# Weight splits of the differential attention made during the retention and kept in DRAM, with small steps moved between engines: a diffusion backbone on one core

## The chip, the cores and the metric

The kernel runs on one core of a Trainium2 chip. The metric is the device time of one execution in microseconds, lower is better. Everything is fp32 at the edges; most matrix products run in the single-pass format fp32r, with each fp32 operand split into two parts.

## The reference, cut to what matters

Two layers work on 512 latent tokens and 256 context tokens of width 1024. Layer 0 mixes tokens by retention, layer 1 by differential attention (8 heads, 512 queries, 768 keys); each is followed by a gated convolutional FFN. The change concerns the attention:

```python
q, k, v = jnp.split(u @ w_in, [D_MODEL, 2 * D_MODEL], axis=-1)     # per head: q1, q2, k1, k2 of 64, v of 128
q1x, q2x = rope_2d(q1x, row, col), rope_2d(q2x, row, col)          # latents only; the same for k1x, k2x
s1 = einsum('bhqd,bhkd->bhqk', q1, k1) * scale;  s2 = einsum('bhqd,bhkd->bhqk', q2, k2) * scale
p = softmax(s1) - lam * softmax(s2)
o = einsum('bhqk,bhkv->bhqv', p, v)
y = merge_heads(rms_norm(o, subln_g) * (1.0 - lam_init)) @ w_out
```

## The kernel before, in words

**Splitting.** An fp32 matrix is written as H + L, both fp32r: ScalarE casts it to H and another engine subtracts to get L (`split`, L58). `mm3` (L96) then makes three products, H·H, H·L and L·H. A weight unit is 128x1024 (512 KB). `W` (L67) loads it into a ring of three raw buffers (`load_raw`, L62, a DMA of the SP queue) and splits it into `wH` and `wL`, rings of two buffers each; the engine of the subtraction is VectorE unless the call names GpSimd.

**Order of the work.** TensorE and SP run in the order in which the program is written; the planner orders ScalarE, VectorE and GpSimd, where weight splits have a raised priority (L72). Weights are asked for where they are used, so SP runs ahead as far as the raw ring lets it.

**Retention (to about 760 us).** For each of four heads: queries and keys by `feat` (L583 on), six token tiles of a gate and of the values by `proj_tok` (L248), the masked scores (L661), and `retain` (L692) for six tiles in each of two directions, with a root of GpSimd in `rsq` (L127). `ada_next` (L544) places units of the modulation among them; they use the same raw ring. Results go to DRAM from the GpSimd queue (L573, L580). Then come the output projection and the FFN of layer 0.

**Attention (about 1430 to 1850 us).** The first head's query and key weights (units 2 and 3 of `diff_in`) are fetched early by `pre_in` (L841). The values of the first pair of heads follow (L912), and then a loop over 36 slots (L1258). A slot makes the scores of one 128-query block of one head (`scores`, L1137), transposes the probabilities of the slot before (`xpose`, L1164) and every second slot multiplies them by the values (`values`, L1177). Between these the loop draws steps from a generator (`filler`, L1073): the projections of the next heads (`qk_steps`, L960, with `q_split`, `k_split` and `kc_split`), the values of the next pair (`v_steps`, L979) and, late, the output projection and the first FFN units. These take weights by `W`; query and value units are subtracted on GpSimd, key units on VectorE.

**Scores.** Queries are held as H in 64 partitions and L in the other 64; keys as `k1`, `k2` (H in both halves) and `l1`, `l2` (L in both halves), so two products of contraction 128 give all four terms. VectorE takes the maxima (`nm`, L1151), ScalarE the two exponentials with their sums (L1156), VectorE a reciprocal, a factor (L1158, L1159) and the mix of both softmaxes (L1161). There is one buffer of scores.

**Norm.** `norm_a` (L1198) squares and sums a head's output per query, `rsq` and small VectorE steps make a factor, four VectorE steps put it on diagonals (`dg`, L1215), and `norm_b` (L1218) spreads it over partitions with a product of `ones` and `dg` in fp32 (`psr`, L1221) and multiplies (`yT`, L1223).

The rotation (`rope`, L866) is a shuffle and two products, then a product with the sine and a sum (L870, L871); for heads up to 6 the calls at L968 and L973 name GpSimd for the sum and, with queries, for the sine product.

Of the kernel before, what the change touches and what calls it, by code (L numbers as in the profile page):

```python
# [18 lines left out]
P = 128  # L19
# [11 lines left out]
def tile_hybrid_backbone(ctx: ExitStack, tc: tile.TileContext, A, out, dbg=None):  # L31
# [35 lines left out]
    class W:  # L67
# [23 lines left out]

        def __call__(self, c, n):
            i, o = divmod(c, self.n)
            return self.H[i][:, o : o + n], self.L[i][:, o : o + n]
# [10 lines left out]
    nc.vector.memset(ones, 1.0)  # L105
    mhalf = cst.tile([P, 8], F32, name="mhalf")
    nc.vector.memset(mhalf, -0.5)

# [37 lines left out]
    gd = dr.tile([8, 8, P], F32, name="gd")  # L146

# [409 lines left out]

    def flush_rows(psp):
        while grows:
            gate_row(psp, *grows.pop(0))  # L560
# [22 lines left out]
    for h in range(4):  # L583
# [3 lines left out]
        for qi in range(2):  # L587
            px = [bank("psqx") for _ in range(2)]
            pc = bank("psqc", (P, 2, 256))
            for c in range(2):  # L590
# [7 lines left out]
                feat(U, w, pc[:, c, :], "c")  # L598
                if prev_y is not None and c == 0:
                    y_out(h - 1, prev_y)  # L600
                    prev_y = None
# [109 lines left out]
        for i in (4, 5, 0, 1, 2, 3):  # L711
            retain(0, i, yg[i])
        if h > 0:
# [171 lines left out]
    def k_split(o, px, eng=None, add=None):  # L885
        kr = rope(px, eng, add)
        o.k1, o.k2 = s2(F32R, name="k1"), s2(F32R, name="k2")
        o.l1, o.l2 = s2(F32R, name="kl1"), s2(F32R, name="kl2")
        for dst, ldst, a in ((o.k1, o.l1, lo), (o.k2, o.l2, hi)):
            for b in (lo, hi):  # L890
                nc.scalar.activation(out=dst[b, :], in_=kr[a, :], func=AF.Copy)
            for b in (lo, hi):
                sub(ldst[b, :], kr[a, :], dst[a, :].bitcast(F32))

    def kc_split(o, pc):
        o.kc, o.klc = s2(F32R, (P, 2, 256), name="kc"), x2("klc", (P, 2, 256))
        for i, a in ((0, lo), (1, hi)):
            for b in (lo, hi):
                nc.scalar.activation(out=o.kc[b, i, :], in_=pc[a, :256], func=AF.Copy)
        for i, a, b in ((0, lo, lo), (0, lo, hi), (1, hi, lo), (1, hi, hi)):  # L900
            sub(o.klc[b, i, :], pc[a, :256], o.kc[a, i, :].bitcast(F32))
# [10 lines left out]
    wv = [W(din[i]) for i in range(2)]  # L912
# [66 lines left out]
    def v_steps(pair, tps=(0, 1, 2)):  # L979
        wv = [W(din[pair * 6 + n], eng=getattr(nc, 'gpsimd')) for n in range(2)]  # L980
# [151 lines left out]
    class Head:  # L1132
# [4 lines left out]
        def scores(self, qt):  # L1137
# [3 lines left out]

            parts = [(o.q1, o.k1[:, :], o.l1[:, :], 0, 512),
                     (o.q1, o.kc[:, 0, :], o.klc[:, 0, :], 512, 256),
                     (o.q2, o.k2[:, :256], o.l2[:, :256], 768, 256),
                     (o.q2, o.k2[:, 256:], o.l2[:, 256:], 1024, 256),
                     (o.q2, o.kc[:, 1, :], o.klc[:, 1, :], 1280, 256)]
            for qd, kd, kl, c, n in parts:
                nc.tensor.matmul(S[:, c : c + n], qd[:, qs], kd, start=True, stop=False)
                nc.tensor.matmul(S[:, c : c + n], qd[:, qs], kl, start=False, stop=True)
# [286 lines left out]
```

## Time and profile before

| | |
|---|---|
| median of 3 runs | 2204.94 us (2198.9 to 2206.59) |
| the profiled execution's own time | 2202.28 us |
| its span | 2200.5 us |
| TensorE busy | 2146.4 us |
| VectorE, ScalarE, GpSimd busy | 1222.3, 843.8, 242.5 us |
| mean granted TensorE clock | 0.989 |

The span runs from the first to the last instruction of the profiled execution. Busy time counts instructions, not waits. PE is TensorE's products, PEld its weight loads, DVE is VectorE, ACT ScalarE, POOL GpSimd and SP the queue engine of the transfers. The ends of matrix products are modelled, since they overlap, so the distance between two starts tells how long one takes in a row of them. The granted clock is a share of the full 2.4 GHz. A row of waits names the engine and line that waited, what ended the wait, and the total, the count and the longest in microseconds.

### The profile page before, as it was taken

How to read it: one execution, taken by the hardware profiler on the slowest of the kernel's cores; microseconds unless marked ns; L12 is line 12 of the kernel's file. 1: busy time of each engine (PE TensorE's matmuls, PEld its weight loads, DVE VectorE, ACT ScalarE, POOL GpSimd, SP SyncE). 2: the span in 40 equal slices, each digit the busy share in tenths (PEclk: the TensorE clock that was granted, in tenths of full speed). 3: DMA queues.
4: the chain of work that ended last, by engine and by line, in shares of the span. 5: the costliest groups of instructions: out<-in, count | busy, mean ns of one | idle time of the engine just before them, and what ended most of it. 6: DMA issues, size and time to landing. Idle time of an engine off the chain costs nothing. (4 is left out here: it accounts for less than half of the span.)

```text
span 2200.5 us, 28121 instructions
## 1 busy us (share of the span) xinstructions
PE 2146.4 (98%) x11096; PEld 1825.0 (83%) x11096; DVE 1222.3 (56%) x1923; ACT 843.8 (38%) x1488; POOL 242.5 (11%) x309
## 2 busy tenths in 40 slices
PE   8999999999999999999999999999999789999998
PEld 5788888888888888888888888888888678888887
DVE  5555553543553348665445625767797676444524
ACT  5432232332332436322222424654455465233422
POOL 3001101100100102000000001021232151000000
PEclk9999999999999999999999999999999899999999
DMA  7222322322223365434434436611110333333333
GB/s 269 100 92 87 130 86 68 121 86 67 101 96 101 115 220 200 140 116 143 129 124 128 146 105 196 212 44 47 43 45 30 115 114 117 98 99 98 108 96 125
DMA packets 82732, 250.68 MB, mean 114 GB/s; under 512 B 10104, under 2 KB 13480, under 8 KB 82472
## 3 DMA queue, kind: packets, MB, share of 16 engines
q1 hardware_dynamic: 79880, 241.00, 33.3%
q0 software_dynamic: 2720, 7.89, 0.9%
q8 instruction: 87, 1.43, 0.3%
q14 instruction: 45, 0.37, 0.1%
HBM read 232.05 MB, written 16.80 MB: 113 GB/s over the span
## 5 line engine op out<-in xcount | busy, mean ns | idle before, releaser
L60 DVE TENSOR_TENSOR wL<-wraw,wH 128x1024 fp32r<-128x1024 f32 x232 | 286.0, 1233 | 504.3 <-ACT wH L59 502.3
L59 ACT ACTIVATE wH<-wraw 128x1024 fp32r<-128x1024 f32 x257 | 271.5, 1058 | 646.1 <-PE psa L99 183.1
L97 PE MATMUL psf<-uxH,wH 128*128 128x512 f32 (+1 forms) x672 | 258.6, 385 | 0.0
L98 PE MATMUL psf<-uxL,wH 128*128 128x512 f32 (+1 forms) x672 | 258.5, 385 | 0.0
L99 PE MATMUL psf<-uxH,wL 128*128 128x512 f32 (+1 forms) x672 | 258.1, 384 | 0.1
L97 PE MATMUL pso<-wH,lxH 128*128 128x512 f32 x432 | 168.3, 390 | 0.5 <-ACT yo L579 0.3
L98 PE MATMUL pso<-wL,lxH 128*128 128x512 f32 x432 | 168.1, 389 | 0.0
L99 PE MATMUL pso<-wH,lxL 128*128 128x512 f32 x432 | 168.1, 389 | 0.0
L99 PEld LDWEIGHTS psf<-uxH,wL 128*128 128x128 f32 x672 | 126.3, 188 | 25.4 <-DVE wL L60 0.3
L97 PEld LDWEIGHTS psf<-uxH,wH 128*128 128x128 f32 x672 | 126.5, 188 | 24.0
L164 DVE CUSTOM_DVE_ANT_0 wraw<-wraw,cb 128x1024 f32<-128x1024 f32 x80 | 97.5, 1222 | 87.5 <-DMA wraw<-in_ada_rest_dram 86.8
L98 PEld LDWEIGHTS psf<-uxL,wH 128*128 128x128 f32 x672 | 126.5, 188 | 23.4
L97 PE MATMUL psa<-wH,uxH 128*128 128x512 f32 x352 | 137.0, 389 | 0.0
L98 PE MATMUL psa<-wL,uxH 128*128 128x512 f32 x352 | 137.0, 389 | 0.0
L99 PE MATMUL psa<-wH,uxL 128*128 128x512 f32 x352 | 136.9, 389 | 0.0
L137 POOL TENSOR_SCALAR st<-st 128x1 f32<-128x1 f32 x42 | 28.7, 684 | 682.3 <-ACT junk L136 681.1
L97 PEld LDWEIGHTS pso<-wH,lxH 128*128 128x128 f32 x432 | 81.1, 188 | 17.8 <-ACT grow L183 0.5
L99 PEld LDWEIGHTS pso<-wH,lxL 128*128 128x128 f32 x432 | 81.1, 188 | 17.0
L99 PE MATMUL psf<-ucH,wL 128*128 128x256 f32 x336 | 95.1, 283 | 0.0
L98 PE MATMUL psf<-ucL,wH 128*128 128x256 f32 x336 | 95.1, 283 | 0.0
L98 PEld LDWEIGHTS pso<-wL,lxH 128*128 128x128 f32 x432 | 81.1, 188 | 16.6
L97 PE MATMUL psf<-ucH,wH 128*128 128x256 f32 x336 | 94.9, 282 | 0.0
(362 smaller groups left out, 5072.2 us busy)
## 6 DMA issues: line engine op xcount, KB each, us to landing
wraw<-in_up_dram SPq DMA_DIRECT2D x88, 512.0 KB, 3.6
wraw<-in_ada_rest_dram SPq DMA_DIRECT2D x80, 512.0 KB, 3.7
wraw<-in_down_dram SPq DMA_DIRECT2D x66, 512.0 KB, 3.6
wraw<-in_ret_in_dram SPq DMA_DIRECT2D x64, 512.0 KB, 3.7
wraw<-in_ret_out_dram SPq DMA_DIRECT2D x32, 512.0 KB, 3.7
wraw<-in_diff_in_dram SPq DMA_DIRECT2D x24, 512.0 KB, 3.6
wraw<-in_ada_dram SPq DMA_DIRECT2D x16, 512.0 KB, 7.1
wraw<-in_diff_out_dram SPq DMA_DIRECT2D x16, 512.0 KB, 3.7
```

The lines of the kernel that those rows point to most:

```text
L59: nc.scalar.activation(out=h, in_=x, func=AF.Copy)
L60: (eng or nc.vector).tensor_tensor(out=l, in0=x, in1=h.bitcast(F32), op=ALU.subtract)
L97: nc.tensor.matmul(ps, l[0], r[0], start=first, stop=False)
L98: nc.tensor.matmul(ps, l[0], r[1], start=False, stop=False)
L99: nc.tensor.matmul(ps, l[1], r[0], start=False, stop=last)
L137: nc.gpsimd.tensor_scalar(out=s[:, 2:3], in0=s[:, 0:1], scalar1=s[:, 1:2], scalar2=EPS, op0=ALU.add, op1=ALU.add)
L164: nc.vector.tensor_tensor_reduce(out=o, in0=raw, in1=cb[:, v, :], scale=1.0, scalar=0.0, op0=ALU.mult, op1=ALU.add, accum_out=adaF[:, laye ...
```

## The change

22 of the 24 units of `diff_in` are no longer loaded and split when the attention needs them. `split_ahead` loads a unit during the retention, splits it by halves on ScalarE and VectorE and writes both parts to DRAM from the GpSimd queue: once in each of four places of the query and key projections (heads 1 to 3) and after three of the six `retain` tiles of the first direction (all heads). The attention gets its units by `W.stored`: two loads by SP straight into `wH` and `wL`. The rest: all of the rotation on VectorE; queries held as H in both halves and L in both halves, keys as H in one half and L in the other; the reciprocal and the factor of the softmax on GpSimd, with a power in place of the reciprocal; the norm's factor without reciprocals, its root by one power on GpSimd; the diagonals in two parts H (ScalarE) and L (VectorE), with two fp32r products in place of one fp32 product.

```diff
+        @classmethod
+        def stored(cls, H, L):
+            w = cls.__new__(cls)
+            w.n = 1024
+            w.H = [wp.tile([P, 1024], F32R, tag="wH", name="wH", bufs=2)]
+            w.L = [wp.tile([P, 1024], F32R, tag="wL", name="wL", bufs=2)]
+            nc.sync.dma_start(out=w.H[0].bitcast(F32), in_=H)
+            nc.sync.dma_start(out=w.L[0].bitcast(F32), in_=L)
+            return w
...
+    split_list = [i for i in range(24) if i not in (2, 3)]
+    def split_ahead(n=1):
+        for _ in range(n):
+            if not split_list:
+                return
+            i = split_list.pop(0)
+            raw = load_raw(A["diff_in"][i])
+            for j in range(2):
+                o = slice(j * 512, j * 512 + 512)
+                H = t2(dt=F32R, name="sH")
+                nc.scalar.activation(out=H, in_=raw[:, o], func=AF.Copy)
+                sub(raw[:, o].bitcast(F32R), raw[:, o], H.bitcast(F32))
+                nc.gpsimd.dma_start(out=dinH[i, :, o], in_=H.bitcast(F32))
+            nc.gpsimd.dma_start(out=dinL[i], in_=raw)
...
                 feat(U, w, pc[:, c, :], "c")
+                if h > 0:
+                    split_ahead()
...
             retain(0, i, yg[i])
+            if i in (0, 2, 3):
+                split_ahead()
...
+    stored = lambda i: W.stored(dinH[i], dinL[i])
...
     def q_split(o, px, eng=None, add=None):
         q = rope(px, eng, add)
-        o.q1, o.q2 = x2("q1"), x2("q2")
-        for dst, h_, l_ in ((o.q1, lo, hi), (o.q2, hi, lo)):
-            nc.scalar.activation(out=dst[h_, :], in_=q[h_, :], func=AF.Copy, scale=0.125)
-            nc.vector.scalar_tensor_tensor(out=dst[l_, :], in0=q[h_, :], scalar=0.125, in1=dst[h_, :].bitcast(F32),
-                                           op0=ALU.mult, op1=ALU.subtract)
+        o.q1, o.q2 = (x2("q1"), s2(F32R, name="ql1")), (x2("q2"), s2(F32R, name="ql2"))
+        for (H, L), a in ((o.q1, lo), (o.q2, hi)):
+            for b in (lo, hi):
+                nc.scalar.activation(out=H[b, :], in_=q[a, :], func=AF.Copy, scale=0.125)
+            for b in (lo, hi):
+                nc.vector.scalar_tensor_tensor(out=L[b, :], in0=q[a, :], scalar=0.125, in1=H[a, :].bitcast(F32),
+                                               op0=ALU.mult, op1=ALU.subtract)
     def k_split(o, px, eng=None, add=None):
         kr = rope(px, eng, add)
         o.k1, o.k2 = s2(F32R, name="k1"), s2(F32R, name="k2")
-        o.l1, o.l2 = s2(F32R, name="kl1"), s2(F32R, name="kl2")
-        for dst, ldst, a in ((o.k1, o.l1, lo), (o.k2, o.l2, hi)):
-            for b in (lo, hi):
-                nc.scalar.activation(out=dst[b, :], in_=kr[a, :], func=AF.Copy)
-            for b in (lo, hi):
-                sub(ldst[b, :], kr[a, :], dst[a, :].bitcast(F32))
+        for dst, a, b in ((o.k1, lo, hi), (o.k2, hi, lo)):
+            nc.scalar.activation(out=dst[a, :], in_=kr[a, :], func=AF.Copy)
+            sub(dst[b, :], kr[a, :], dst[a, :].bitcast(F32))
     def kc_split(o, pc):
-        o.kc, o.klc = s2(F32R, (P, 2, 256), name="kc"), x2("klc", (P, 2, 256))
...
+        o.kc = s2(F32R, (P, 2, 256), name="kc")
+        for i, a, b in ((0, lo, hi), (1, hi, lo)):
+            nc.scalar.activation(out=o.kc[a, i, :], in_=pc[a, :256], func=AF.Copy)
+            sub(o.kc[b, i, :], pc[a, :256], o.kc[a, i, :].bitcast(F32))
...
-    wv = [W(din[i]) for i in range(2)]
+    wv = [stored(i) for i in range(2)]
...
-        w = W(din[wi], eng=getattr(nc, 'gpsimd'))
+        w = stored(wi)
...
-            q_split(o, ps, *((getattr(nc, 'gpsimd'), getattr(nc, 'gpsimd')) if hd < 7 else ()))
-        w = W(din[wi + 1], eng=getattr(nc, 'vector'))
+            q_split(o, ps)
+        w = stored(wi + 1)
...
-            k_split(o, ps, *((getattr(nc, 'vector'), getattr(nc, 'gpsimd')) if hd < 7 else ()))
+            k_split(o, ps)
...
-        wv = [W(din[pair * 6 + n], eng=getattr(nc, 'gpsimd')) for n in range(2)]
+        wv = [stored(pair * 6 + n) for n in range(2)]
...
+            for (qh, ql), kd, c, n in parts:
+                nc.tensor.matmul(S[:, c : c + n], qh[:, qs], kd, start=True, stop=False)
+                nc.tensor.matmul(S[:, c : c + n], ql[:, qs], kd, start=False, stop=True)
...
-            nc.vector.reciprocal(out=nm[:, 3:4], in_=nm[:, 2:3])
-            nc.vector.scalar_tensor_tensor(out=nm[:, 4:5], in0=nm[:, 3:4], scalar=self.sums[:, qt : qt + 1], in1=nlam,
-                                           op0=ALU.mult, op1=ALU.mult)
+            nc.gpsimd.tensor_tensor(out=nm[:, 3:4], in0=nm[:, 2:3], in1=mone, op=ALU.pow)
+            nc.gpsimd.tensor_scalar(out=nm[:, 4:5], in0=nm[:, 3:4], scalar1=self.sums[:, qt : qt + 1], scalar2=nlam,
+                                    op0=ALU.mult, op1=ALU.mult)
...
-            nc.vector.reciprocal(out=r[:, 0:m], in_=sums)
-            nc.vector.tensor_tensor(out=r[:, 4 : 4 + m], in0=pn[:, 0:m], in1=r[:, 0:m], op=ALU.mult)
-            nc.vector.tensor_tensor(out=r[:, 4 : 4 + m], in0=r[:, 4 : 4 + m], in1=r[:, 0:m], op=ALU.mult)
-            rsq(r[:, 8 : 8 + m], r[:, 4 : 4 + m], P, m)
-            nc.vector.tensor_tensor(out=r[:, 8 : 8 + m], in0=r[:, 8 : 8 + m], in1=r[:, 0:m], op=ALU.mult)
-            self.dg = s2(shape=(P, 4, P), name="dg")
+            nc.gpsimd.tensor_tensor(out=r[:, 0:m], in0=sums, in1=sums, op=ALU.mult)
+            nc.vector.scalar_tensor_tensor(out=r[:, 4 : 4 + m], in0=r[:, 0:m], scalar=EPS, in1=pn[:, 0:m],
+                                           op0=ALU.mult, op1=ALU.add)
+            nc.gpsimd.tensor_tensor(out=r[:, 8 : 8 + m], in0=r[:, 4 : 4 + m], in1=mhalf[:, :m], op=ALU.pow)
+            self.dg = [s2(F32R, (P, 4, P), name=n) for n in ("dgH", "dgL")]
             for i in range(m):
...
+                nc.scalar.activation(out=H, in_=ident, func=AF.Copy, scale=f)
+                nc.vector.scalar_tensor_tensor(out=L, in0=ident, scalar=f, in1=H.bitcast(F32), op0=ALU.mult, op1=ALU.subtract)
...
-            nc.tensor.matmul(pr[:, :n], ones, self.dg.rearrange("p a b -> p (a b)")[:, :n], start=True, stop=True)
+            for i, x in enumerate(self.dg):
+                nc.tensor.matmul(pr[:, :n], onesr, x.rearrange("p a b -> p (a b)")[:, :n], start=i == 0, stop=i == 1)
```

## Rows read from the trace of the kernel before

**Rows 1.** Page, part 1: busy us, share of the span and instructions of each engine.

```profile
PE 2146.4 (98%) x11096; PEld 1825.0 (83%) x11096; DVE 1222.3 (56%) x1923; ACT 843.8 (38%) x1488; POOL 242.5 (11%) x309
```

**Rows 2.** Windows: stretch, length, busy PE PEld DVE ACT POOL, clock, DMA share, GB/s.

```profile
150.00:760.00 610.00, 609.18 (x2893) 511.92 (x2892) 302.55 (x483) 193.21 (x340) 64.14 (x136) 1.00 0.28 94
...
1462.00:1715.00 253.00, 239.84 (x1560) 216.61 (x1560) 199.68 (x318) 132.48 (x255) 68.51 (x46) 0.97 0.15 49
1715.00:1850.00 135.00, 112.05 (x636) 94.96 (x635) 99.75 (x176) 73.78 (x159) 44.07 (x37) 0.90 0.36 125
```

**Rows 3.** Waits of TensorE over the whole span.

```profile
PE pso L97 <- DVE klc L56: 6.0, 1, 6.0
PE pspt L1172 <- DVE E L1161: 4.5, 5, 2.4
PE psn L1203 <- DVE yT L1223: 4.2, 4, 1.7
...
PE psv L97 <- DVE klc L56: 2.7, 3, 2.4
```

**Rows 4.** Windows of 10 us, the slice where TensorE idles longest.

```profile
1720.00:1730.00 10.00, 2.51 (x11) 1.71 (x12) 9.79 (x15) 6.67 (x15) 2.35 (x1) 0.62 0.28 79
```

**Rows 5.** Timeline, VectorE and GpSimd, 1721 to 1726 us: start, us, what.

```profile
1721.22 4.85 DVE L56 TENSOR_TENSOR kl<-dr,k 64x512 fp32r<-64x512 f32 x4
...
1722.47 2.35 POOL L60 TENSOR_TENSOR wL<-wraw,wH 128x1024 fp32r<-128x1024 f32 x1 [8.70 <-ACT wH L59]
```

**Rows 6.** VectorE groups by shape, 1440 to 1850 us; one with min/median/max ns.

```profile
L56 DVE TENSOR_TENSOR kl<-dr,k 64x512 fp32r<-64x512 f32 x32 | 29.5, 923 | 1.6 <-ACT k L891 1.3
...
L60 DVE TENSOR_TENSOR wL<-wraw,wH 128x1024 fp32r<-128x1024 f32 x15 | 18.2, 1220 | 4.5 <-ACT wH L59 4.3
...
L56 DVE TENSOR_TENSOR klc<-pskc,kc 64x256 fp32r<-64x256 f32 x32 | 13.5, 421 | 3.5 <-ACT kc L899 3.1
...
L1159 DVE SCALAR_TENSOR_TENSOR nm<-nm,sums,nlam 128x1 f32<-128x1 f32 x32 | 10.6, 332 | 0.7
...
L1158 DVE RECIPROCAL nm<-nm 128x1 f32<-128x1 f32 x32 | 5.1, 160 | 10.4 <-ACT E L1156 10.3
...
L56 DVE TENSOR_TENSOR kl<-dr,k x32: 670/687/2800, 1449.4 to 1725.4; 64x512 fp32r<-64x512 f32 x32
```

**Rows 7.** GpSimd's write issues in the retention: ns of one, and us to landing.

```profile
L573 POOL DMA_DIRECT2D yTd<-yo x16: 539/539/770, 230.3 to 744.0; - x16
...
yTd<-yo POOLq DMA_DIRECT2D x16, 256.0 KB, 4.8
```

**Rows 8.** Timeline of ScalarE, head 1 of the retention.

```profile
322.99 1.06 ACT L59 ACTIVATE wH<-wraw 128x1024 fp32r<-128x1024 f32 x1 [7.05 <-PE psa L99]
...
345.43 0.60 ACT L707 ACTIVATE junk<-pso 128x512 bf16<-128x512 f32 x1 [3.39 <-PE pso L99]
```

**Rows 9.** GpSimd's one-column steps of the layer norm, 1440 to 1850 us, min/median/max ns.

```profile
L137 POOL TENSOR_SCALAR st<-st x8: 453/896/1499, 1803.7 to 1844.7; 128x1 f32<-128x1 f32 x8
...
L138 POOL TENSOR_TENSOR st<-st,mhalf x8: 557/715/924, 1804.9 to 1845.4; 128x1 f32<-128x1 f32 x8
```

**Rows 10.** Timeline of TensorE at the first values, the first query unit, a norm.

```profile
1459.07 0.28 PE L99 MATMUL psv<-wH,ucL 128*128 128x256 f32 x1
...
1462.07 0.40 PE L97 MATMUL psq<-uxH,wH 128*128 128x512 f32 x1
1462.30 0.40 PE L98 MATMUL psq<-uxL,wH 128*128 128x512 f32 x1
1462.97 0.50 PE L99 MATMUL psq<-uxH,wL 128*128 128x512 f32 x1 [0.27 <-POOL wL L60]
...
1564.52 1.02 PE L1221 MATMUL psr<-dg,ones 128*128 128x512 f32 x2
```

**Rows 11.** Transfers: the retention's units; two loads at 1703 us; all raw loads, 1440 to 1850 us.

```profile
wraw<-in_ret_in_dram SPq DMA_DIRECT2D x64, 512.0 KB, 3.7
...
wraw<-in_diff_out_dram SPq DMA_DIRECT2D x2, 512.0 KB, 4.3
...
DMA to landing us min/median/max: 3.3/3.7/5.7
```

More of the change, by code (lines that the diff above doesn't have):

```diff
@@ L105, in tile_hybrid_backbone @@
     nc.vector.memset(ones, 1.0)
+    onesr = cst.tile([P, P], F32R, name="onesr")
+    nc.scalar.activation(out=onesr, in_=ones, func=AF.Copy)
     mhalf = cst.tile([P, 8], F32, name="mhalf")
     nc.vector.memset(mhalf, -0.5)
+    mone = cst.tile([P, 1], F32, name="mone")
+    nc.vector.memset(mone, -1.0)
     csil = cst.tile([P, KT, 2], F32, name="csil")
@@ L146, in tile_hybrid_backbone @@
     gd = dr.tile([8, 8, P], F32, name="gd")
+    dinH = dr.tile([24, P, 1024], F32, name="dinH")
+    dinL = dr.tile([24, P, 1024], F32, name="dinL")
     x_in, ctx_in = A["x"], A["ctx"]
@@ L1140, in scores @@
             S = bt("s3", "s3", (P, 1536))
[L1142 to L1149, printed above, removed]
+            parts = [(o.q1, o.k1[:, :], 0, 512), (o.q1, o.kc[:, 0, :], 512, 256), (o.q2, o.k2[:, :256], 768, 256),
+                     (o.q2, o.k2[:, 256:], 1024, 256), (o.q2, o.kc[:, 1, :], 1280, 256)]
+            for (qh, ql), kd, c, n in parts:
+                nc.tensor.matmul(S[:, c : c + n], qh[:, qs], kd, start=True, stop=False)
+                nc.tensor.matmul(S[:, c : c + n], ql[:, qs], kd, start=False, stop=True)
             nm = st(name="nm")
@@ L1194, in values @@
                 self.sq = t2(name="sq")
-                nc.scalar.activation(out=self.sq[:, : self.n], in_=self.po[:, : self.n], func=AF.Square)
+                nc.scalar.activation(out=self.sq[:, : self.n], in_=self.po[:, : self.n], func=AF.Square, scale=P ** -0.5)
         def norm_a(self):
@@ L1204, in norm_a @@
             r = st(16, name="rr")
-            nc.vector.reciprocal(out=r[:, 0:m], in_=sums)
-            nc.vector.tensor_tensor(out=r[:, 4 : 4 + m], in0=pn[:, 0:m], in1=r[:, 0:m], op=ALU.mult)
-            nc.vector.tensor_tensor(out=r[:, 4 : 4 + m], in0=r[:, 4 : 4 + m], in1=r[:, 0:m], op=ALU.mult)
-            rsq(r[:, 8 : 8 + m], r[:, 4 : 4 + m], P, m)
-            nc.vector.tensor_tensor(out=r[:, 8 : 8 + m], in0=r[:, 8 : 8 + m], in1=r[:, 0:m], op=ALU.mult)
-            self.dg = s2(shape=(P, 4, P), name="dg")
-            for i in range(m):
-                if 'vector' == "scalar":
-                    nc.scalar.activation(out=self.dg[:, i, :], in_=ident, func=AF.Copy, scale=r[:, 8 + i : 9 + i])
-                else:
-                    getattr(nc, 'vector').tensor_scalar(out=self.dg[:, i, :], in0=ident, scalar1=r[:, 8 + i : 9 + i],
-                                                        scalar2=None, op0=ALU.mult)
+            nc.gpsimd.tensor_tensor(out=r[:, 0:m], in0=sums, in1=sums, op=ALU.mult)
[3 more added lines that the diff above has]
+            self.dg = [s2(F32R, (P, 4, P), name=n) for n in ("dgH", "dgL")]
+            for i in range(m):
+                H, L = (x[:, i, :] for x in self.dg)
+                f = r[:, 8 + i : 9 + i]
+                nc.scalar.activation(out=H, in_=ident, func=AF.Copy, scale=f)
+                nc.vector.scalar_tensor_tensor(out=L, in0=ident, scalar=f, in1=H.bitcast(F32), op0=ALU.mult, op1=ALU.subtract)
         def norm_b(self):
@@ L1262, in tile_hybrid_backbone @@
             if hd not in heads:
-                while hd not in qks or not hasattr(qks[hd], "klc"):
+                while hd not in qks or not hasattr(qks[hd], "kc"):
                     fill(1)
```

5 lines of the change are left out of this document (removed).

## Prediction

> **What bounds the kernel now.** I read the page first: TensorE is busy for 98% of the span [rows 1], so the change can win only what TensorE loses by waiting or by running slowly. The windows by stage come next [rows 2]. They show that the retention (150 to 760 us) leaves 0.8 us of TensorE idle, while the attention's 36 slots lose 253.0 - 239.8 = 13.2 us up to 1715 us and 135.0 - 112.1 = 22.9 us up to 1850 us: 36 us in all. The same rows hold the second loss: the granted clock averages 0.97 and 0.90 there, which is at most 253 x 0.03 + 135 x 0.10 = 21 us, less what of it falls into idle time. So about 57 us, 2.6% of the run, is all that ending waits can win. After 1850 us both kernels run the same code.
>
> Then TensorE's waits [rows 3]: those for `klc` (the split of the context keys, which frees a PSUM bank) make 6.0 + 2.7 = 8.7 us, those for `E` (the mixed softmax) 4.5 us, those for the norm's `yT` 4.2 us. VectorE ends all of these, and in the slice where TensorE idles longest, 1720 to 1730 us, VectorE is busy for 9.79 of 10 us [rows 4]; that slice was granted 0.62, between the clock's two levels of 2.4 and 1.2 GHz. Some of VectorE's time is GpSimd's doing: four key splits take 4.85 us beside a weight split of 2.35 us on GpSimd [rows 5], where one alone takes 0.69 us at the median and 2.80 at most [rows 6].
>
> **The change, part by part.** *Splits moved to the retention.* 22 pieces, each one load on SP, two casts on ScalarE, two subtractions on VectorE (0.69 us, the 512-column split of [rows 6]) and three write issues on GpSimd (0.54 us each, landed after 4.8 us, [rows 7]): 22 x 1.38 = 30 us of VectorE in a stretch where it is busy 303 of 610 us, and 22 x 1.6 = 36 us of GpSimd, busy 64 [rows 2]. What they could delay is a weight of the retention, because a piece holds one of three raw buffers from its load until its write has landed: about 3.7 [rows 11] + 2.6 + 4.8 = 11 us. The tightest place is the three pieces ahead of a head's second gate projection. Its first unit is cast at 322.99 us, and TensorE reaches it only after the sixth retained tile, whose square starts at 345.43 [rows 8]. Some 22 us of cover stand against 11 to 15 us; I take 0. If the cover were 4 us short in each of three heads, 12 us would be lost: the upper bound. A gain is excluded, since TensorE has none to give there. GpSimd's reciprocal roots queue behind the write issues; the projection of four units that follows hides them.
>
> *VectorE in the attention.* It loses 9 weight splits (two for the first values, seven for keys) x 1.22 = 11.0 us, 16 of 32 key splits x 0.92 = 14.8, 16 of 32 context-key splits x 0.42 = 6.7, the 64 softmax factors (5.1 + 10.6 = 15.7) and a few small norm steps; it gains 18 rotation steps and 16 query splits x 0.69 = 23.5 us [rows 6]. Net 48 - 24 = 24 us less, and some 7 us more by the norm steps, of 299 us busy [rows 2]. GpSimd loses 13 weight splits (31 us by the row of 2.35) and all rotation, which also takes away most of what lengthens VectorE's steps (the mean of `kl` is 0.92, its median 0.69: 7 us there alone). ScalarE loses 22 casts of whole weight units, swaps key casts for query casts and gets 32 small diagonal blocks; nothing in [rows 3] waits for it, so 0.
>
> On TensorE: behind the wait of 6.0 us stood four key splits (4.85 us) and four context splits (4 x 0.42); these become 1.4 and 0.85, so over 4 us go, and more of the others: 7.5 of 8.7 us. For `E` I take 2 of 4.5 us, because its factor becomes slower (below); for `yT` 2.5 of 4.2, since the norm loses some VectorE steps but keeps GpSimd's power. Of the other 19 us (exponentials, accumulators, last norms) 3. Together 15 of 36 us. By proportion 15/36 of the clock loss goes with them, 9 us; part of that lies in idle time, so I take 7.
>
> *Softmax factors on GpSimd.* Now 0.16 + 0.33 us on VectorE [rows 6]. The trace has no such pair on GpSimd; the nearest are the layer norm's one-column steps, 0.90 and 0.72 us at the median, 0.45 and 0.56 at least [rows 9]. So the pair costs 1.0 to 1.6 us; I take 1.2, 0.7 us more than now. The wait that it adds stands on VectorE, in front of `E`; splits of keys and probabilities queue behind it there. `E` is consumed one slot later (a slot is 388 / 36 = 10.8 us), so the delay is hidden except in the slots already late; that is in the 2 of 4.5 above.
>
> *Diagonal in two parts.* The fp32 product of 512 columns (two passes) takes 1.02 us to its end; two single products take 0.23 + 0.40 = 0.63, by the first two query products [rows 10]. That saves 0.4 x 6 + 0.2 x 4 = 3 us.
>
> *Loads of stored weights.* This is the cost. Now a raw unit waits on the chip and only the split follows the release of its buffer: the last read of such a buffer ended at 1459.07 + 0.28, and the third product of the first query unit, which needs both halves, started at 1462.97 [rows 10]: 3.6 us. Afterwards two loads follow the release. Two loads in a row landed after 4.3 us in the median; the longest of the stretch took 5.7 [rows 11]. Per unit that is 0.7 to 2.1 us later; I take 0.9, nearest to the pair. SP stands meanwhile with everything behind it: the next units and, late, the loads and stores of the output projection, which have over 10 us. TensorE needs a unit at once in seven places: the first query, the second half of the values (three times), the query that follows values (three times); elsewhere a whole slot lies between. 7 x 0.9 = 6 us, from 5 to 15. *Key and query swapped in the scores:* as many products of the same size, 0.
>
> **Sum.** 15 (waits) + 7 (clock) + 3 (diagonal) - 6 (loads) = 19 us less. The profiled execution took 2202.28 us (span 2200.5), 2.7 below the median of 2204.94, so 2183 for it and 2186 as a median. Low bound: three quarters of the idle (27 us), 13 of the clock and 3, with the loads hidden: 2162. High bound: 4 of waits, 3 of clock and 3 gained, 15 lost on loads: 2210.
>
> **Rivals.**
> *1, all VectorE waits vanish.* With a tenth less work, and GpSimd's long steps gone, each slot has room. For it: VectorE is full just where TensorE waits. Against: the tail's waits are for other things. 27 + 10 + 3 - 1 = 39 us: about 2166.
> *2, the factor eats the relief.* A GpSimd step that meets a VectorE step is slow: up to 1.50 us where the shortest takes 0.45 [rows 9]. If the pair takes 2.4 us (1.50 + 0.92), 1.9 more than now, and the five slots that wait for `E` become seven, 13 us of the gain go: 2199. Against it: GpSimd's long steps are some 57 us fewer. A page has a rule that leads here: the Trainium skill (SBUF — State Buffer, "SBUF: two separate sides") says that a VectorE step with two SBUF inputs and a GpSimd step exclude each other for a whole instruction. By that rule the 64 new short steps would queue for the port behind splits and mixes and hold those up in turn. The trace agrees that the engines delay each other (the 2.80 us split).
> *3, stored loads come too late (slower).* If the pair lands after the 5.7 us, each of the seven places waits 2.1 us, and the lower clock adds up to 21/36 of that, 1.2 us: 23 us; if TensorE then waits so at the other 13 units too, each by half, 21 us more. Of the gain 25 us stay: 2205 + 44 - 25 = 2224. It turns slower once the loads cost more than 25 us, 1.3 us for each of 20 units. Against it: DMA is at a share of 0.15 in that stretch [rows 2], and outside the seven places a slot lies between release and use.
> *4, the retention is delayed*, by its bound of 12 us: 2198. It counts with rival 2, since both end near no change.
>
> **How the numbers follow.** Forecast 0.55, rival 1 0.16, rivals 2 and 4 together 0.17, rival 3 0.12. A measurement of this kernel can tell about 0.5% (11 us) from no change. Faster than 2194 are rival 1 and nearly all of the forecast, 0.67; slower than 2216 is rival 3 and a little of the rest, 0.13; the remaining 0.20 is the same. The range, 2162 to 2209, takes in the forecast with its bounds and rivals 1, 2 and 4, and leaves out rival 3 and the end of rival 1.
>
> **What would show it.** Right: TensorE's idle in the attention falls from 36 to about 25 us, with the `klc` waits nearly gone; VectorE is busy for 30 to 50 us less there; new waits of some 1 us at the first products of `psq` or `psv`, released by a load of stored weights; the stretch up to 880 us unchanged within 3 us; `psr` in two products of 0.39 us. Wrong: waits of over 3 us on stored weights, more waits for `E`, or TensorE idle between 150 and 760 us.

## The result, and the profile after

The changed kernel takes 2243.2 us (median of 6 runs, 2240.44 to 2248.63) where the kernel before takes 2203.89; the ratio is 1.0181 (95% interval 1.0165 to 1.0198). That is 39 us slower, where 19 us faster was forecast, and above the range. The profiled execution took 2240.44 us with a span of 2238.7, 38.2 us more than before. Line numbers after are higher: the three products of `mm3` are L108 to L110, a piece's cast is L587, its writes are L589 and L590.

The busy times barely moved. The page of the changed kernel, part 1, against [rows 1]:

```profile
PE 2148.7 (96%) x11096; PEld 1823.8 (81%) x11096; DVE 1213.6 (54%) x1867; ACT 852.8 (38%) x1528; POOL 250.8 (11%) x408
```

TensorE is busy for 2 us more in a span that is 38 us longer: over the whole run nearly all of the difference is idle time. The windows by stage say where; the first line answers to the first of [rows 2], the other two are slices of 25 us in it:

```profile
150.00:760.00 610.00, 582.34 (x2721) 486.09 (x2720) 311.76 (x503) 200.61 (x353) 92.49 (x182) 0.98 0.43 143
...
225.00:250.00 25.00, 17.23 (x108) 14.99 (x106) 16.65 (x26) 7.74 (x14) 10.42 (x16) 0.86 0.68 233
...
600.00:625.00 25.00, 17.91 (x86) 14.82 (x85) 15.02 (x23) 9.85 (x17) 7.48 (x14) 0.80 0.68 236
```

In the retention TensorE is idle for 27.7 us (0.8 before), in a few places, and the granted clock falls there: these two slices were granted 0.86 and 0.80, a mixture of the levels of 1.2 and 2.4 GHz, where the kernel before has 1.00. What the lower clock costs shows up to the first product of the attention's values, before and after:

```profile
0.00:1441.80 1441.80, 1430.43 (x7155) 1205.94 (x7156) 764.47 (x1230) 515.45 (x903) 125.05 (x218) 1.00 0.39 129
```

```profile
0.00:1479.90 1479.90, 1440.94 (x7157) 1209.93 (x7157) 787.91 (x1274) 541.22 (x948) 162.46 (x284) 0.99 0.46 149
```

The same products keep TensorE busy for 10.5 us more, and its idle time grows by 27.6 us (11.4 to 39.0). The waits of TensorE in the whole span name what it waits for:

```profile
PE psqx L108 <- ACT wH L59: 17.4, 3, 6.4
PE pso L108 <- DVE kc L56: 10.5, 1, 10.5
PE psqx L110 <- DVE wL L60: 5.5, 4, 1.7
...
PE psa L108 <- ACT wH L59: 3.3, 2, 1.8
```

`psqx` is the retention's query and key projection and `psa` its gates and values: in every head after the first, TensorE waits for the weight of the keys. The second row lies in the attention and answers to the first of [rows 3].

The starts of a few products split the run into stages. They come from the tile views of the three kernels (the first values; the last H·H product of the last head's queries, `psq`; the last transpose of the FFN's input, `pst`; the last product), the last row from the spans:

| us | before | after | without storage (below) |
|---|---|---|---|
| first `psv` | 1441.8 | 1479.9 | 1442.2 |
| first `psv` to last `psq` | 262.4 | 251.1 | 253.2 |
| last `psq` to last `pst` | 145.4 | 151.9 | 154.0 |
| last `pst` to last product | 343.9 | 343.8 | 343.9 |
| last product to the end | 7.0 | 12.0 | 7.0 |

All of the loss, 38.1 us, is there before the attention begins. The attention wins 11.3 us early and gives 6.5 back late; 5.0 more are lost at the very end of the program.

How the retention loses shows in its transfers. The timeline of SP after, end of head 0 (start, us from the first issue to the end of the last, what):

```profile
173.72 4.60 SPq L64 DMA_DIRECT2D wraw<-in_diff_in_dram  x3
202.95 8.00 SPq L64 DMA_DIRECT2D wraw<-in_ada_rest_dram  x2
211.04 0.40 SPq L64 DMA_DIRECT2D wraw<-in_ret_in_dram  x1
...
226.13 7.00 SPq L64 DMA_DIRECT2D wraw<-in_ada_rest_dram  x2
242.69 0.33 SPq L64 DMA_DIRECT2D wraw<-in_ret_in_dram  x1
```

and ScalarE at the same time:

```profile
192.64 0.60 ACT L743 ACTIVATE junk<-pso 128x512 bf16<-128x512 f32 x1
...
196.58 1.14 ACT L587 ACTIVATE sH<-wraw 128x512 fp32r<-128x512 f32 x2
...
202.76 1.14 ACT L587 ACTIVATE sH<-wraw 128x512 fp32r<-128x512 f32 x2
...
206.84 1.14 ACT L587 ACTIVATE sH<-wraw 128x512 fp32r<-128x512 f32 x2
```

SP runs ahead and fills all three raw buffers with pieces by 178 us. ScalarE takes them where they stand in its order, between the squares of the retained tiles (L743), from 196.58 us on, and a buffer comes free only when its write has landed: SP's next load starts at 202.95. A buffer was held for 29.2 us, not 11. The next head's four projection units, the third of them the first of its keys, come late in turn, but this hold alone does not make TensorE wait for the keys: with these pieces and no others (`e3_retain_places`, below) SP issues that key unit at 224.40 us, and TensorE does not stand for it.

What stands in front of the key unit in the changed kernel is the second piece of the query projection. ScalarE:

```profile
230.58 1.09 ACT L605 ACTIVATE yo<-psy 128x512 f32<-128x512 f32 x2 [4.96 <-PE psy L603]
231.55 2.08 ACT L613 ACTIVATE yo<-psy 128x512 f32<-128x512 f32 x4
235.43 0.63 ACT L587 ACTIVATE sH<-wraw 128x512 fp32r<-128x512 f32 x1 [1.80 <-DMA yTd<-yo]
237.60 0.63 ACT L587 ACTIVATE sH<-wraw 128x512 fp32r<-128x512 f32 x1 [1.54 <-DMA yTd<-yo]
```

SP issues this piece at 221.87 us. ScalarE casts it behind the outputs of the head before (`yo`), and each cast waits for a write of `yo` as well, because both use the ring `t2`. The buffer is free 20.8 us after the issue, at 242.69, when its write has landed (SP waits 9.4 us for that write), and the key unit is the load that needs it. SP of the kernel before issues that key unit here:

```profile
210.31 0.33 SPq L64 DMA_DIRECT2D wraw<-in_ret_in_dram  x1
```

which is 29 us before its first product (239.32 us). In the changed kernel it is the load at 242.69 us, and TensorE waits 6.4 us for its cast. The view that sums this up is that of SP's own waits. From 150 to 780 us, of the kernel before:

```profile
SPq L64 <- DVE wL L60: 365.7, 58, 21.3
```

and after:

```profile
SPq L64 <- DVE wL L60: 207.2, 49, 21.3
SPq L64 <- DMA dinL<-wraw: 195.0, 19, 24.6
```

Before, SP stood for 366 us because the three buffers were full of weights that had come early: that standing was the stage's lead. After, it stands 195 us for pieces' writes, and its standing for weights has fallen by 159 us (366 to 207).

### The profile page after: what moved, and what is told of

It is laid out like the page before. It is cut to its first block, busy times and chain, and to the rows that moved or that the text cites. A ratio compares the mean times of both kernels' runs of the same rounds, so it can differ in the third digit from the quotient of the medians.

```text
span 2238.7 us, 28412 instructions
## 1 busy us (share of the span) xinstructions
PE 2148.7 (96%) x11096; PEld 1823.8 (81%) x11096; DVE 1213.6 (54%) x1867; ACT 852.8 (38%) x1528; POOL 250.8 (11%) x408
## 5 line engine op out<-in xcount | busy, mean ns | idle before, releaser
L60 DVE TENSOR_TENSOR wL<-wraw,wH 128x1024 fp32r<-128x1024 f32 x223 | 275.0, 1233 | 464.7 <-ACT wH L59 460.4
L59 ACT ACTIVATE wH<-wraw 128x1024 fp32r<-128x1024 f32 x235 | 248.2, 1058 | 576.1 <-PE pso L110 167.8
L108 PE MATMUL psf<-uxH,wH 128*128 128x512 f32 (+1 forms) x672 | 258.7, 385 | 0.0
L110 PE MATMUL psf<-uxH,wL 128*128 128x512 f32 (+1 forms) x672 | 258.1, 384 | 0.2 <-DVE wL L60 0.2
L108 PE MATMUL pso<-wH,lxH 128*128 128x512 f32 x432 | 168.3, 390 | 0.5 <-ACT yo L613 0.3
L110 PE MATMUL pso<-wH,lxL 128*128 128x512 f32 x432 | 168.1, 389 | 0.0
L110 PEld LDWEIGHTS psf<-uxH,wL 128*128 128x128 f32 x672 | 126.3, 188 | 25.7 <-DVE wL L60 0.4
L108 PEld LDWEIGHTS psf<-uxH,wH 128*128 128x128 f32 x672 | 126.4, 188 | 23.7
L108 PE MATMUL psa<-wH,uxH 128*128 128x512 f32 x352 | 137.2, 390 | 3.3 <-ACT wH L59 3.3
L110 PE MATMUL psa<-wH,uxL 128*128 128x512 f32 x352 | 137.0, 389 | 0.0
L108 PEld LDWEIGHTS pso<-wH,lxH 128*128 128x128 f32 x432 | 81.1, 188 | 17.7 <-ACT grow L200 0.5
L110 PE MATMUL psf<-ucH,wL 128*128 128x256 f32 x336 | 95.1, 283 | 0.0
L108 PE MATMUL psf<-ucH,wH 128*128 128x256 f32 x336 | 94.9, 282 | 0.0
L109 PEld LDWEIGHTS pso<-wL,lxH 128*128 128x128 f32 x432 | 81.1, 188 | 16.9
L110 PEld LDWEIGHTS pso<-wH,lxL 128*128 128x128 f32 x432 | 81.1, 188 | 16.9
```

Source lines behind the costliest of these rows:

```text
L59: nc.scalar.activation(out=h, in_=x, func=AF.Copy)
L60: (eng or nc.vector).tensor_tensor(out=l, in0=x, in1=h.bitcast(F32), op=ALU.subtract)
L108: nc.tensor.matmul(ps, l[0], r[0], start=first, stop=False)
L109: nc.tensor.matmul(ps, l[0], r[1], start=False, stop=False)
L110: nc.tensor.matmul(ps, l[1], r[0], start=False, stop=last)
```

## The experiments

**Which part costs.** `e1_no_store` is the changed kernel with no unit stored (the attention loads and splits all its units, queries and values on GpSimd, as before); `e2_store_alone` is the kernel before with the storage alone.

```diff
-    split_list = [i for i in range(24) if i not in (2, 3)]
+    split_list = []
+    ready = list(split_list)
...
-    stored = lambda i: W.stored(dinH[i], dinL[i])
+    stored = lambda i, eng=None: W.stored(dinH[i], dinL[i]) if i in ready else W(din[i], eng=eng)
```

> The changed kernel without its storage: no piece is split in the retention, all 24 units go through raw buffers and splits in the attention as before (query and value units subtracted on GpSimd, key units and the first values on VectorE); the other parts of the change stay. Theory A (the pieces in the retention cost 38 us, the attention gains some 5): TensorE idles under 2 us between 150 and 760 us, and the median is 2192 to 2202 us. Theory B (the small steps on GpSimd and VectorE are themselves what costs, the storage only part of it): slower than before, over 2210.

> The kernel before plus the storage alone (pieces split in the retention, stored units loaded in the attention); rotation, queries, softmax factors and norm as before. Theory A: the retention is 35 to 40 us longer as in the changed kernel, the attention within 8 us of before: 2235 to 2250 us. Theory B: 2205 to 2220.

Measured: 2201.86 us without storage, ratio to the kernel before 0.9994 (0.9985 to 1.0004), and 2242.83 us with storage alone, 1.0177 (1.0154 to 1.0201), both inside Theory A's ranges. The storage is the whole loss, and everything else in the change is worth nothing that can be measured. The second finding is a miss of its own, since the forecast's gain lay in the lighter attention.

**Which places cost.** Twelve units are stored, either after the retained tiles of all four heads (`e3_retain_places`) or in the query and key projections of heads 1 to 3 (`e4_qk_places`); the attention splits the others itself.

```diff
-                if h > 0:
-                    split_ahead()
...
-    split_list = [i for i in range(24) if i not in (2, 3)]
+    split_list = [i for i in range(24) if i not in (2, 3)][:12]
```

(this is `e3`; `e4` leaves out the call after `retain` instead)

> The changed kernel with pieces only after the retained tiles (12 units stored), the other units split in the attention as before. Theory A, with the cost where TensorE idles in the changed kernel's windows: these places stand behind the idle of some 2.5 us per head at the second gate projection, so the retention loses 5 to 12 us; 2200 to 2212. If each piece costs the same wherever it stands: half of 38, about 19 us lost.

> The changed kernel with pieces only in the query and key projections (12 units stored), the other units split in the attention as before. Theory A: these places stand behind the idle of 7 us and the low clock at the key projection of heads 1 to 3, so the retention loses 22 to 32 us; 2218 to 2232. If each piece costs the same wherever it stands: about 19 us.

Measured: 2215.2 us (1.006, 1.0041 to 1.0078) and 2231.4 us (1.0126, 1.011 to 1.0141). The first values start 14.2 and 29.5 us late: inside what Theory A gave for `e4`, 2 to 3 us above it for `e3`. The losses above the kernel before, 12 and 28, add up to the whole one, and a piece does not cost the same in the two places. Nor does TensorE wait for the same weights. In `e3`, from 150 to 780 us, the gates' come late and the keys' do not:

```profile
PE psa L108 <- ACT wH L59: 6.2, 3, 3.1
PE psa L109 <- DVE wL L60: 2.3, 3, 0.8
```

and in `e4` only the keys':

```profile
PE psqx L108 <- ACT wH L59: 16.1, 3, 5.7
PE psqx L110 <- DVE wL L60: 4.5, 3, 1.8
```

There the second piece of the first query projection is issued at 210.48 us and still cast at 234.20, behind the outputs of the head before; the key unit follows at 240.78. So the waits for keys, the larger part of the loss, belong to the projections' pieces.

**Late casts.** `e5_raised` wraps the steps of a piece in the raised priority that weight splits have.

```diff
-            for j in range(2):
...
+            with tc.high_priority(offset=AHEAD):
+                for j in range(2):
```

> The changed kernel with the 22 pieces' casts, subtractions and write issues at a raised priority, like the weight splits, so that ScalarE takes a piece when its load has landed and not at its place in the program. Theory A (a piece holds a raw buffer for some 35 us because ScalarE reaches its cast late): the loss of 38 us before the first values falls under 12 us, and the time to 2203 to 2218 us. Theory B (the loss comes with the extra transfers and the engine time of the pieces, however early they are taken): it stays within 6 us of 2243. Theory D (SP and the ring are the limit, since each piece still puts one more load of 4 us and one more release into the same three buffers): half of the loss stays, 2218 to 2230.

Measured: 2246.15 us (1.0197). This decides nothing: the casts stand at the same places in ScalarE's order (196.4, 202.6 and 206.6 us), so what was to be changed did not change: with the raised priority the planner put them at the places where they had stood.

**Another place.** `e6_in_ffn` takes both calls out of the retention and puts a piece after every second modulation unit of layer 0's FFN and the rest behind it.

```diff
+    def between():
+        ada_next()
+        if ada_at[0] % 2 == 0:
+            split_ahead()
...
-    F = FFNUp(psp, u, 0, True, ada_next)
+    F = FFNUp(psp, u, 0, True, between)
```

> The changed kernel with the pieces moved out of the retention: about one after every second modulation unit of the first layer's FFN, the rest after it. Theory A (only the place, where a ring of three raw buffers feeds the retention just in time, costs): no TensorE idle in the retention beyond the 0.8 us of before; the FFN loses under 8 us; 2195 to 2210 us. Theory B (splitting and writing 22 units costs TensorE time anywhere): over 2225.

Measured: 2231.35 us (1.0137, 1.012 to 1.0153), the number of Theory B (over 2225). Of Theory A only its first part held: the retention is as before (609.17 of 610 us busy), but the first values come 26.7 us late. TensorE's waits of that run between 760 and 1470 us:

```profile
PE psf L110 <- DVE wL L60: 9.1, 11, 1.9
PE pso L108 <- ACT wH L59: 8.1, 1, 8.1
```

The FFN is fed by the same three buffers and has little more room than the retention. That the ring is the cause here too was not tried.

**The ring, from four sides.** `e7_four_raw` adds a fourth raw buffer (and takes two from `t2` for the room). `e9_lower_apart` subtracts into two tiles of `t2` and writes from there, so that the raw buffer is free after the subtraction. `e10_no_write` loads and splits the pieces but writes nothing, and the attention splits its own units. `e8_early` places a head's three pieces right after its last value weight, and those of the projections ahead of the products. The cuts below are of `e7`, `e9` and `e8`, in this order; `e7` also sets the ring `t2` from 6 to 4.

```diff
-        raw = s6(name="wraw")[:, :1024] if big else wp.tile([P, 1024], F32, tag="wraw", name="wraw", bufs=3)
+        raw = s6(name="wraw")[:, :1024] if big else wp.tile([P, 1024], F32, tag="wraw", name="wraw", bufs=4)
...
-                sub(raw[:, o].bitcast(F32R), raw[:, o], H.bitcast(F32))
+                L = t2(dt=F32R, name="sL")
+                sub(L, raw[:, o], H.bitcast(F32))
...
-        proj_tok(psp, U, [win[w0 + 8 + i] for i in range(4)], (4, 5, 0, 1, 2, 3), split_v)
-        ada_next(3)
+        proj_tok(psp, U, [win[w0 + 8 + i] for i in range(4)], (4, 5, 0, 1, 2, 3), split_v, hook=lambda: (ada_next(3), split_ahead(3)))
```

> The changed kernel with a fourth raw buffer (its room is taken from the ring t2, four buffers in place of six, which by itself can only cost). Theory D (the three raw buffers are the limit: each piece occupies one for 11 us or more, and SP takes all loads in order): the loss of 38 us before the first values falls below 15 us, the time to 2225 or less. Theory B (the extra transfers and the engine time of the pieces cost, whatever the ring): within 6 us of 2243, or slower.

> The changed kernel with the same order on SP inside a projection, but with the three pieces of the retained tiles placed right after the last value weight, so that ScalarE casts them before it evacuates the values and not between the retained tiles; pieces of the query and key projections one product group earlier. Theory A (late casts hold the buffers): the 12 us of the retained tiles' places go, and the time falls to 2228 to 2235. Theory D (a piece occupies a raw buffer for its own load, split and write, and there are too few): less than 5 us is gained, 2238 or more.

> The changed kernel with the lower part of a piece subtracted into two t2 tiles and written from there (four writes of half a unit instead of three), so that the raw buffer comes free with the subtraction and not with the end of the write, some 5 us earlier of 11 or 12. The engine work and the bytes are the same. Theory D: a third to a half of the 28 us of the projections' places goes, 2225 to 2235, unless the t2 ring takes the raw ring's place. Theory B: within 5 us of 2243.

> The 22 pieces are loaded and split in the retention, but not written, and the attention loads and splits its weights from the input as the kernel before does; so it is the kernel without storage (2202) plus the loads and splits of the pieces. Theory D: a raw buffer is held for some 7 us in place of 12, so half of the 38 us or less is lost, 2212 to 2224. Theory B with the loads or the engine steps as the cause: 2236 or more. If the writes alone are the cause: 2202 to 2206.

| | us | ratio, interval | first values late by | idle of 610 us |
|---|---|---|---|---|
| the change | 2243.2 | 1.0181 (1.0165 to 1.0198) | 38.1 | 27.7 |
| `e7_four_raw` | 2223.9 | 1.0099 (1.0084 to 1.0114) | 23.6 | 11.9 |
| `e8_early` | 2238.3 | 1.0163 (1.0144 to 1.0183) | 33.6 | 22.9 |
| `e9_lower_apart` | 2234.4 | 1.0144 (1.0129 to 1.016) | 33.9 | 20.9 |
| `e10_no_write` | 2222.2 | 1.0091 (1.0076 to 1.0107) | 18.7 | 11.8 |

The fourth buffer takes some half of the loss away (19 us of 39; 14.5 of the 38.1 before the first values) with all loads, splits and writes still there: for that half the number of buffers is the cause, and not the traffic or the engines' work. (The time is what Theory D gave; the delay of the first values is above its 15 us, and 6.7 us of it arise after the retention, where the smaller `t2` may count: the first product of the output projection is 16.9 us late.) The first key unit of head 1 is issued at 229.22 us there, and TensorE does not wait for it.

Without writes (`e10`) half of the delay goes as well, as Theory D gave, but the earlier release of the raw buffers explains only a small part of it. `e9` frees them at the same step, after the subtraction, and SP stands as long for the pieces in both runs (`e9`, then `e10`, 150 to 780 us):

```profile
SPq L64 <- DVE sL L56: 158.6, 22, 20.8
```

```profile
SPq L64 <- DVE wraw L56: 158.2, 22, 20.8
```

Yet `e9` takes only 4.2 of the 38.1 us away, where Theory D expected a third to a half of 28; its time lies in the forecast because the end of the program became 4.8 us shorter (last section). The other 15 us between `e9` and `e10` come with the writes and the `t2` buffers that they hold (four for a piece in `e9`, two in the change). In `e9` the pieces' steps wait 16.3 us for writes of `yo` and 5.1 for those of `sH` (6.9 and none in the change), which is the exception that the expectation named. How much of the 15 us is the traffic was not separated.

The idle that is left in `e7` is another thing. In the waits of that run the cast has nearly gone, and the subtraction stands in its place:

```profile
PE psqx L110 <- DVE wL L60: 9.9, 3, 3.7
...
PE psqx L108 <- ACT wH L59: 0.8, 1, 0.8
```

VectorE was busy from 240.5 to 254.8 us without a gap, modulation products, the queries' rotation and the pieces' subtractions in front of the key weight's split (251.81 us). `e8` gains 5 us and stands at the edge of Theory D's range (2238 or more): its slice from 350 to 375 us is full again (25.00 busy, 22.48 in the change), the waits of `psa` for a cast weight are gone, but the projections' pieces cost as before (`psqx` still waits 15.5 us, and the second of them is still cast behind the outputs, at 233.47 us). `e13_early_only` then takes the twelve early pieces alone.

> The kernel of the twelve pieces among the retained tiles (2215 us, the first values 14 us late), but with the three pieces of a head placed right after its last value weight, so that ScalarE can cast them before the retained tiles. Theory A (there the buffers are held by late casts): no wait for a weight in the gate projections, the first values at most 3 us late, and 2198 to 2204 us. Theory D (three buffers are too few for twelve more loads): the first values stay 8 us or more late, 2209 or more.

Measured: 2210.86 us (1.004, 1.0026 to 1.0054), the first values 10.1 us late: the numbers of Theory D, 4 us better than late casts (`e3`), but not by its cause. SP's next load now starts at 185.37 us and not at 202.95, and the waits for a weight are gone. What TensorE waits for instead:

```profile
PE pso L108 <- ACT vH L722: 4.1, 2, 2.2
...
PE pso L109 <- DVE vL L56: 2.6, 3, 0.9
```

The three pieces now stand in front of the values' evacuation on ScalarE and VectorE. Neither of the two places tried is free: taken late they block the ring, taken early they block the evacuation.

**Why the lighter attention gains nothing.** Its early part is 9.2 us shorter in the run without storage, and 11.8 us with the storage alone (250.6 us from first `psv` to last `psq`). Either relief of VectorE is enough for it, and the two do not add up. Its late part is longer in both (154.0 and 149.9 us against 145.4). In the run without storage the longest wait is the one for `kc`, 10.4 us (with storage 10.5, before 6.0 for `klc`). VectorE of the changed kernel at that point:

```profile
1743.55 0.67 DVE L907 TENSOR_TENSOR dr<-psk,dcos 128x512 f32<-128x512 f32 x1
1744.14 2.57 DVE L60 TENSOR_TENSOR lxHL<-yin,lxHL 128x256 fp32r<-128x256 f32 x1
1746.63 1.00 DVE L1195 SCALAR_TENSOR_TENSOR E<-E,nm 128x768 f32<-128x768 f32 x1
1747.56 2.58 DVE L60 TENSOR_TENSOR lxHL<-yin,lxHL 128x256 fp32r<-128x256 f32 x1
...
1755.95 1.40 DVE L56 TENSOR_TENSOR k<-dr,k 64x512 fp32r<-64x512 f32 x2
...
1759.22 0.43 DVE L56 TENSOR_TENSOR kc<-pskc,kc 64x256 fp32r<-64x256 f32 x1
```

and GpSimd:

```profile
1744.05 2.38 POOL L60 TENSOR_TENSOR wL<-wraw,wH 128x1024 fp32r<-128x1024 f32 x1 [0.87 <-ACT wH L59]
1747.04 2.82 POOL L60 TENSOR_TENSOR wL<-wraw,wH 128x1024 fp32r<-128x1024 f32 x1 [0.61 <-ACT wH L59]
```

The last keys' splits are cheap now (1.40 us for two, 4.85 for four in [rows 5]), but two splits of attended values stand ahead of them in VectorE's order and each ends just after a weight split on GpSimd. `e11_last_keys` moves those splits behind the keys in the program; `e12_late_dve` gives the two weight splits to VectorE. Both start from `e1_no_store`.

```diff
-                if hd == 7 and i in (20, 24, 28):
-                    lt_of(0, i // 4 - 5)
...
+            if hd == 7:
+                for j in range(3):
+                    lt_of(0, j)
```

```diff
-            wahead.append(W(*src, eng=nc.gpsimd if nw[0] in (6, 19, 15, 1, 2, 10, 14, 3, 12, 7, 13) else None))
+            wahead.append(W(*src, eng=nc.gpsimd if nw[0] in (6, 19, 15, 10, 14, 3, 12, 7, 13) else None))
```

> The kernel without storage (2201.9 us), with the first three splits of attended values for the output projection moved in the program behind the last head's key splits; before, they stood between the steps of that head's keys. Theory P (the small steps gain nothing because the planner put the last keys behind two such splits, which take 2.6 us each beside GpSimd's weight splits: TensorE waits 10.4 us for kc): the wait falls to 3 to 6 us and the time to 2194 to 2198, faster than before by 0.2 to 0.4%. Theory Q (the output projection's first products need those splits as soon as the bank is free, so the wait only changes its name): 2200 to 2204.

> The kernel without storage (2201.9 us), with the first two weight splits of the output projection on VectorE and not on GpSimd. If the two engines exclude each other there (a split of 128x256 takes 2.6 us on VectorE while GpSimd works, 0.42 otherwise), VectorE loses 4.4 us of delay and gains two splits of 1.22: the wait for kc falls from 10.4 to 7 to 9 us, the time to 2198 to 2201. If they do not, the splits stay at 2.6 us and the time goes up by 2 us.

Measured: 2200.66 us (0.9989, 0.998 to 0.9998) and 2199.17 us (0.9984, 0.9975 to 0.9993). In `e11` the wait for `kc` is 0.4 us, and a wait of 4.7 us for the moved split's cast stands in its place, as the second theory had it; the gain of 1 us is a miss for the first. In `e12` the same two splits take 0.43 us each:

```profile
1708.81 0.43 DVE L60 TENSOR_TENSOR lxHL<-yin,lxHL 128x256 fp32r<-128x256 f32 x1
1709.14 1.02 DVE L1196 SCALAR_TENSOR_TENSOR E<-E,nm 128x768 f32<-128x768 f32 x1
1710.07 0.43 DVE L60 TENSOR_TENSOR lxHL<-yin,lxHL 128x256 fp32r<-128x256 f32 x1
```

and the waits of TensorE, 1440 to 1860 us:

```profile
PE pso L109 <- DVE wL L60: 7.0, 3, 3.3
PE pso L108 <- DVE kc L56: 4.7, 1, 4.7
PE s L1183 <- ACT E L1191: 4.5, 4, 1.5
```

The wait for `kc` falls by 5.7 us; that for a weight's lower part rises from 3.3 to 7.0, and 2.7 us are left as a gain, inside the time expected, with a shorter wait than expected and a new one beside it. `e14_early_dve` does the same on top of the twelve early pieces.

> The kernel before this one in the list, with the first two weight splits of the output projection on VectorE. If the late wait for the last keys is what keeps the attention from gaining: 3 us less than that kernel, and, with Theory A there, 2195 to 2200, faster than the kernel before by 0.1 to 0.4%. If other waits take its place as in the kernel without storage: within 1 us of that kernel.

Measured: 2208.07 us (1.0024, 1.0015 to 1.0033), 2.8 less than `e13`: the step is worth the same there. The 2195 to 2200 hung on free early pieces, which `e13` does not have. `e12_late_dve` is the fastest kernel of the study: the small steps of the change without its storage, with two weight splits taken off GpSimd, 0.16% faster than the kernel before.

## Why the prediction was wrong

**Splits in the retention: 0 us forecast, 38 measured.** This is the step that failed. It had the right resource (three raw buffers) and the wrong price and place. "A piece holds one of three raw buffers from its load until its write has landed: about 3.7 + 2.6 + 4.8 = 11 us" leaves out the time between landing and cast: SP issues a load as soon as a buffer is free, ScalarE casts at the place in its own order, and 29.2 us lay between issue and release behind the retained tiles of head 0, 20.8 us at the second piece of the next query projection. The cover was then read at one place only, the gate projection after the retained tiles, "the tightest place", as "22 us of cover against 11 to 15". That place did come late (`psa`, 3.3 us for the cast), and the pieces there cost 14.2 us when they stand alone (`e3`). The four pieces in a head's projections had no cover read at all, and they cost more: 29.5 us alone (`e4`), by the waits at the key projection (`psqx`, 17.4 us for the cast in the change). The bound of 12 us (rival 4) rested on the same price and the same one place; SP's own waits, which show the lead that the pieces use up, did not enter it. What of the loss does not go with a fourth buffer is shown only in part: VectorE's order (`e7`) and the writes (`e9` against `e10`) have a share, and their sizes stay open.

"A gain is excluded" was right, and so was the last sign on the list of what would show the forecast wrong: TensorE idle between 150 and 760 us.

**VectorE's load: right, and without effect in sum.** 24 and 7 us less were forecast for the attention; from first `psv` to last `pst` VectorE is busy 312 us before and 280 after. But of TensorE's idle 15 us were to go, and it rose by 3: 36.1 us before (407.8 - 371.7 busy, from first `psv` to last `pst`), 39.4 after (403.0 - 363.6). Early waits did go: up to the last `psq` the idle fell from 13.2 to 9.3 us, new waits for stored units included, and the other 7.4 of the 11.3 us won there are busy time. Late, the idle rose from 22.9 to 30.1 us. The forecast's largest single term, 7.5 of 8.7 us for `klc`, failed: the step that stood in front of the last keys was taken to be their own long splits, while behind them two others would run into GpSimd. GpSimd's late weight splits were not among those that the change removes.

**The clock and the diagonal.** 7 and 3 us were forecast; the busy time of TensorE in this stretch fell by 8.1 us, 371.7 to 363.6, which holds both. It is close to the sum of 10, and the only gain that stays. With the storage alone (`e2`), where the diagonal is as before, 6.0 us of it are there too (365.7), so the clock has the larger share.

**Stored loads: 6 us forecast, 4.5 measured** (four rows of TensorE's waits on `wH<-dinH` and `wL<-dinL`, the longest 1.8). Rival 3, the slower one, did not occur; the time lies above its 2224 by another mechanism.

**Softmax factors.** The pair takes 0.62 + 0.37 us in the mean (1.2 taken), and waits for `E` did not grow in number. Rival 2 did not occur at the factor. Its mechanism did, in another place: the 2.6 us splits above. The Trainium skill (SBUF — State Buffer, "SBUF: two separate sides") has such a VectorE step excluded for the whole of a GpSimd instruction; the trace agrees, 2.57 and 2.58 us beside GpSimd and 0.43 without it.

**The end.** That the last 350 us stay as they are was right up to the last product (343.9 and 343.8 us), but 5 us came after it.

## What to carry to other kernels

Before work is put into a stretch that looks idle by its busy shares, look at the wait of the transfer queue there: a queue that stands because its buffers are full is the stage's lead, and whatever borrows a buffer spends that lead for everything behind it. The sum of that standing is a warning, not a price (SP stood 265 us for weights in `e4` and 237 in `e10`, with 20.6 and 11.8 us of TensorE's idle). Price the borrowed buffer from the issue of its load to its release in the order of the slowest engine that touches it, not by the sum of its own steps, and at every place where one is borrowed: the place that looked tightest here cost less than the one that was not read. And when an engine is relieved, ask which of the steps left stands in front of the one that is waited for: the order decides, not the load.

## What the runs showed of the hardware

The end of the program became longer with what was stored. SP waits there for TensorE's queue after the last output store; the rows of the change, of `e3_retain_places` and of `e9_lower_apart`:

```profile
SPq L1466 <- PEq L1466: 5.9, 2, 5.4
```

```profile
SPq L1465 <- PEq L1465: 3.2, 2, 2.7
```

```profile
SPq L1467 <- PEq L1467: 1.1, 2, 0.9
```

The longest wait is 5.4 us in all runs with 22 stored units and writes of 512 KB from the raw buffers, 2.7 in those with 12 such units, 0.9 with 22 units in writes of 256 KB (`e9`), and 0.5 to 0.6 without writes. It follows the writes and not the loads of the stored units, but which part of them it follows was not tried, and its cause is open.
